# S5 increments as quarter-array products without a zero-padded token copy

## The chip, the cores and the metric

The program runs on one core of a Trainium2 chip. The metric is the device time of one execution in microseconds (us). Five engines work side by side, each through its own queue in order: TensorE (PE, with its weight loads shown apart as PEld), VectorE (DVE), ScalarE (ACT), GpSimd (POOL) and SyncE (SP, which here only issues transfers). PE's array has 128 rows (the contraction) and 128 columns (the rows of the output). A matmul that uses 64 of either leaves the rest to others: in the rows below `128*64` is a matmul that holds a stationary block of 128 rows and 64 columns, and `64*128` one of 64 rows and 128 columns.

## What is computed

Two network blocks run over 256 tokens of width 2048: an attention block with two layers, then a block whose mixer is a linear recurrence (S5). The part that matters:

```python
def s5_scan(u, lam_bar, b_bar, s0, reverse):
    bu = jnp.einsum('btgh,gph->btgp', u, b_bar)
    first = -1 if reverse else 0
    bu = bu.at[:, first].add(lam_bar * s0)
    a = jnp.broadcast_to(lam_bar, bu.shape)
    _, states = lax.associative_scan(_lin_rec_combine, (a, bu), axis=1, reverse=reverse)
    return states

def s5_mixer(h_ctx, h_lat, ...):
    u_ctx, u_lat = to_groups(h_ctx), to_groups(h_lat)
    ...
    for direction in range(2):
        st_ctx = s5_scan(uc_ctx, lam_bar, b_bar, s0, reverse)
        s_ctx_final = st_ctx[:, 0] if reverse else st_ctx[:, -1]
        st_lat = s5_scan(uc_lat, lam_bar, b_bar, s_ctx_final, reverse)
        y_lat = y_lat + jnp.einsum('btgp,ghp->btgh', st_lat, c_mat).real
```

Each of the 128 groups has 16 input features and 64 complex states, in two directions. The kernel takes four tokens together as a chunk (64 chunks in 256 tokens). A chunk's contribution to the state, its **increment**, is a product of 64 inputs (four tokens of 16 features) with a table of the group: 64 rows, and 64 states for each direction and for the real and the imaginary part. The recurrence then runs over the 64 chunks.

## The kernel before

Weights stream through SBUF in tiles of 128 columns, split into two parts (ACT makes `wh`, line 130; DVE makes `wl`, line 131), and are multiplied in three products (lines 156 to 158). The framework's scheduler sets the order of the instructions on every engine from its own model of their times, so an edit in one place can move instructions elsewhere.

The increments are made twice, both times by `chunk_inputs` (line 654), which handles a half block of 8 groups (a block is 16 groups; two tiles, `s` = 0 and 1, of 8 groups each, lie in the rows 0 to 63 and 64 to 127).

- **The context** (`ctx_states`, line 1245): a side job, cut into pieces that run between the weight tiles of the second attention layer, at 1036 to 1361 us of the profile. Eight blocks; in each, ACT scales the context's tokens into `ub` (line 1281, 16 instructions of 64x64), two half blocks of increments are made (line 665, table `wc`), ACT takes them out of PSUM (line 1289), and DVE folds the 64 chunks together (lines 1303 to 1306).
- **The latent tokens** (`s5_mix`, line 1312): at 1384 to 1600 us. The eight blocks are grouped in segments `S0` (blocks 0 and 1), `S1` (2 and 3), `S2` (4 and 5), `S3` (6) and `S4` (7). For each block the layer norm's last step (lines 1078, 1079) and the modulation (lines 1351 to 1353) give `u`; `to_chunks` (line 635) turns it on PE (lines 642 and 648, with copies at line 644 between) into `o2`, copies `o2` from PSUM to SBUF in two halves (line 651) and sends each half on by a DMA of SP (line 652); `chunk_inputs` makes the increments (line 665, table `wl`), and they are copied into the segment's state `S` (line 1363).

Then the recurrence runs in place on `S`, three instructions per chunk (lines 1380 to 1382): segment `S1` on POOL, the others on DVE, from `S0` on. A segment whose recurrence has ended is copied by ACT into `sn` (lines 1433, 1434) and multiplied with the output table (line 1439), on top of the products inside a chunk (line 1408); gelu, and a transposition (line 1470) follow, and then the GLU's weight tiles. The vector-matrix products of the modulations (line 195 on PE, line 210 on DVE, tiles `graw`) fill gaps throughout.

Before the change the increments use all 128 rows of the array: the tokens lie in `ub[128, 8, 2, 64]`, where for the rows of one tile the columns of the other are zero, so that one product gives both tiles' groups side by side:

```python
u = Ub[:, 4 * q + i]
nc.tensor.matmul(inc[ri][r, i], w[:, i, ri, r], u[:, :, ::-1] if d else u, start=True, stop=True)
```

One such matmul moves 128 columns (2 tiles, 64 chunks), half of whose inputs are zero. There are 16 in a half block: 4 group pairs `i`, 2 parts `ri`, 2 directions `d`. The two directions use the two column halves of the array. The profile counts two records for each of these matmuls, so a half block is `x32`. `inc[ri]` is one PSUM bank per part.

Of the kernel before, what the change touches and what calls it, by code (L numbers as in the profile page):

```python
# [11 lines left out]
F32 = mybir.dt.float32  # L12
# [89 lines left out]
def bc(ap, n):  # L102
    """ap [p, m] seen as [p, m, n], each element repeated n times."""
    return bass.AP(tensor=ap.tensor, offset=ap.offset, ap=[list(d) for d in ap.ap] + [[0, n]])


class K:
# [41 lines left out]
    def mm_t(self, a, order=range(KT)):  # L149
        """[128 columns, 256 tokens] of the next column tile; a[kt] = both parts of [128, 256]."""  # L150
# [10 lines left out]
    def mm_n(self, a, half):  # L161
        """[128 tokens, 2, 256 columns]: half 0 opens the sum with the first 8 kt, half 1 closes it."""
# [17 lines left out]
    def gemv(self, w, width, seg, c, outs, biases):  # L180
        """Generator: outs[i][128, 16] = c[i] @ w[:, 2048 seg:] + biases[i]; each step loads a chunk of 1 MB and
        yields the function that adds it, on the engine that send() names."""
# [63 lines left out]
    def step(self):  # L246
        """One step of the first side job."""
        while self.side and next(self.side[0], True):
            self.side.pop(0)
# [5 lines left out]
    def bg_add(self, *jobs):  # L255
        """Queue (name, generator): the first halves of all, then the second."""
        for _, gen in jobs:
            next(gen)
        self.bgq += [(name, gen, 8) for name, gen in jobs] * 2

    def policy(self, engines, split):
        """The engines that add the chunks, and which halves of the weights GpSimd splits."""
        self.pol = itertools.cycle(engines)
        self.spl = itertools.cycle(split)

    def bg(self, n=1, eng=None):
        """n steps of the vector products: each loads a chunk and adds the one before."""
# [25 lines left out]
    def rsqrt(self, v):  # L293
        """v[128, n] (positive) -> v ** -0.5: a guess from the exponent, a step of Newton's and one of Halley's."""
# [5 lines left out]
        # y = 3/8 of the better guess  # L300
# [9 lines left out]
    def spread(self, col, name="rb"):  # L310
        """col[128 tokens, n, 2] -> PSUM [128, n, 256], the value of each token in every partition."""
# [11 lines left out]
    def colsum(self, ps, src, first, last, cols=None):  # L323
        """ps[128 tokens, 2, n] += src[128, 256].T @ cols[128, n] (cols: ones)."""
# [6 lines left out]
    def bands(self, name):  # L331
        """PSUM [128, 256] of zeros for band()."""
# [7 lines left out]
    def band(self, g, q, cols, src):  # L340
        """Rows 32 q .. of g += cols[128, n].T @ src[128, 256]."""
# [3 lines left out]
    def band_sums(self, g, sel, name):  # L345
        """PSUM [128 tokens, 2, n]: the rows of g that sel[128, n] picks and adds."""
# [20 lines left out]
    def small_bg(self, out, a, b, c, d):  # L367
        """a * (1 + b) and c * (1 + b) + d (without c: d), by halves."""
# [16 lines left out]
    def affine_split(self, src, S, B, dst, js=range(KT)):  # L385
        """dst(kt) = both parts of src(kt) * S + B."""
# [13 lines left out]
    def s5_exp(self, x, t, em1=False):  # L400
        """x, t: lists of [128, 128] scratch; returns exp(x) (or exp(x) - 1) in t[0]."""
# [19 lines left out]
    def cmul(self, o, a, b, t):  # L421
        """complex pairs: o = a * b; t: four scratch tiles."""
# [12 lines left out]
    def s5_compact(self):  # L435
# [25 lines left out]
        # w = (lambda_bar - 1) / a  # L461
# [15 lines left out]
        # powers  # L477
# [5 lines left out]
        # factors of the tables by half blocks: [hb, table (W, V), ri, 8 groups, 4 tokens]  # L483
# [17 lines left out]
        # chunk decay and its squarings, per group ((re, im), (-im, re))  # L501
# [12 lines left out]
    def s5_prod(self, t, xr, xi, lr, li, part):  # L514
        """t = the two products of part 0 (real) or 1 (imaginary) of x * l, x [128, n, 16], l [128, n, 4]."""
# [9 lines left out]
    def s5_inputs_table(self, W):  # L525
        """Generator over half blocks (8 groups): the table W from a chunk's tokens to its state, in the
        workspace W[128, 4096]."""
# [39 lines left out]
    def s5_outputs_table(self, W):  # L567
        """Generator over half blocks: the tables V from a chunk's state to its outputs and M inside a
        chunk, in the workspace W[128, 4096]."""
# [4 lines left out]
        # C A^|lag| of 4 groups by lag -3 .. 3, zero where the lag is the other direction's  # L574
# [60 lines left out]
    def to_chunks(self, us, Ub, U, uc, dve=False):  # L635
        """us: two of [128 d, 256 tokens] -> U[128 (tile, tau, h), 8 groups, 64 chunks] (if any), and apart for
        the two tiles in Ub[128, 8 groups, 2, 64], whose other half is zero; uc(q): scratch [64, 4, 2, 64]."""
# [11 lines left out]
        for s in range(2):  # L649
            rows = slice(64 * s, 64 * s + 64)  # L650
            (v.tensor_copy if dve and s else nc.scalar.copy)(Ub[rows, :, s], o2[rows])
            nc.sync.dma_start(U[rows], Ub[rows, :, s])

    def chunk_inputs(self, w, Ub, q, evac):
        """w[128 (s, tau, h), 4, 2, 128 (dir, state)], Ub[128, 8, 2, 64], group pairs 4q .. 4q+3:
        evac(ri, psum[128, 8, 64]), the second direction's chunks backwards."""
# [3 lines left out]
        for i in range(4):  # L660
            for ri in range(2):
                for d in range(2):
                    r = slice(64 * d, 64 * d + 64)
                    u = Ub[:, 4 * q + i]
                    nc.tensor.matmul(inc[ri][r, i], w[:, i, ri, r], u[:, :, ::-1] if d else u, start=True, stop=True)  # L665
        for ri in range(2):
            evac(ri, inc[ri].rearrange("p i s c -> p (i s) c"))

# [77 lines left out]
    def consts(self):  # L746
# [17 lines left out]
        # the first of 32 columns  # L764
# [5 lines left out]
        self.ub = cp.tile([128, 8, 2, 64], F32, name="ub")  # L770
        nc.gpsimd.memset(self.ub, 0.0)
        # one-hot rows p % 16
        self.e16 = cp.tile([128, 16], F32, name="e16")
        nc.vector.tensor_reduce(self.e16, self.idn.rearrange("p (c h) -> p h c", h=16), axis=AX.X, op=ADD)
        # silu of the conditions
# [16 lines left out]
        # one-hot rows that pick the four bands of a vector product  # L792
# [10 lines left out]
        # lambda of the differential attention  # L803
# [10 lines left out]
        # distances s - t, with the future far away  # L814
# [161 lines left out]
    def ctx_rms(self):  # L976
        """1/rms of the context's tokens in the order of its chunks: rx[(tile, tau, h), chunk]."""
# [22 lines left out]
    def out_norm(self, o_, gate, ln, rms=False):  # L1000
        """x <- (z - mean) / std of z = alpha x + gate * (o @ w_out), summed about the mean of the first half
        of the features; with rms also PSUM [128, 256] of 1/rms of the layer norm's output."""
# [3 lines left out]
        if rms:  # L1006
            mw = self.vt.tile([128, KT, 3], F32, name="mw")           # 1, g^2, g b
            mq = self.vt.tile([128, 3, KT], F32, name="mq")           # g^2, g b, b^2
# [55 lines left out]
        if rms:  # L1064
            # sum of (g (w - m) r + b)^2
# [18 lines left out]
    def layer1(self):  # L1084
# [12 lines left out]
        def forget():  # L1097
            """Fs: both parts of the sums F of the log forget gates; nid: columns that pick -F of a head; FT: F's
            transpose."""
# [145 lines left out]
    def ctx_states(self, S, B):  # L1245
        """Generator: the context's last states, by blocks of 16 groups."""
# [7 lines left out]
        # scale and shift of the features in the order of the chunks' rows  # L1254
# [18 lines left out]
        for b in range(8):  # L1273
# [4 lines left out]
            for i in range(8):  # L1278
                for s in range(2):
                    r = slice(64 * s, 64 * s + 64)  # L1280
# [424 lines left out]
```

## Time and profile before

| | |
|---|---|
| time, median of 3 runs (lowest to highest) | 2597.3 us (2597.07 to 2597.63) |
| span of the profiled execution | 2600.7 us |
| PE busy | 2397.3 us (92%) |
| DVE busy | 1755.7 us (68%) |
| ACT busy | 1255.6 us (48%) |
| POOL busy | 209.7 us (8%) |

The span of the profiled execution lies 3.4 us (0.13%) above the median of the timed runs. Busy shares are means over stages that differ much: PE is nearly always busy while weight tiles are multiplied, and much less while the recurrence runs. What a change is worth is therefore read stage by stage, from a table of busy times in windows, and along the chain of work.

### The profile page before, as it was taken

What the parts mean: (1) busy time and instruction counts of PE and PEld (TensorE: products, weight loads), DVE (VectorE), ACT (ScalarE), POOL (GpSimd) and SP (SyncE); (2) the same over time, 40 slices, a digit from 0 to 9 for tenths busy, and PEclk for the clock granted to TensorE, in tenths of its full rate; (3) what the DMA queues carried; (4) which work ended last, traced back from release to release, by engine and by line L of the source; (5) the groups of instructions that cost most, each with busy time, mean ns of one, the idle gap of its engine ahead of it and who ended that gap; (6) DMA issues with size and microseconds to landing.
All of it is one profiled execution on the core that took longest, in us unless ns stands there. A gap on an engine that the chain in (4) does not pass through costs nothing.

```text
span 2600.7 us, 52283 instructions
## 1 busy us (share of the span) xinstructions
PE 2397.3 (92%) x20998; PEld 2172.4 (84%) x20998; DVE 1755.7 (68%) x3223; ACT 1255.6 (48%) x2178; POOL 209.7 (8%) x432
## 2 busy tenths in 40 slices
PE   5699999999899999999997445999899999999997
PEld 1299999999688888898886335998899999999996
DVE  3287878868766555788778998876754554555554
ACT  1455544444365565766555155544544443443442
POOL 0000000000011110000000853000000000000000
PEclk9699999999899999999998766999899999999998
DMA  9999999878779998788776543996355555555552
GB/s 330 343 337 318 333 329 329 317 253 326 252 248 339 333 328 289 264 279 283 258 232 204 182 165 120 331 318 238 119 184 183 184 184 182 186 180 186 182 179 94
DMA packets 203332, 644.92 MB, mean 248 GB/s; under 512 B 41009, under 2 KB 49457, under 8 KB 202705
## 3 DMA queue, kind: packets, MB, share of 16 engines
q1 hardware_dynamic: 195616, 620.47, 69.3%
q0 software_dynamic: 7472, 21.11, 2.1%
q8 instruction: 164, 2.69, 0.4%
q14 instruction: 80, 0.65, 0.1%
HBM read 613.71 MB, written 25.69 MB: 246 GB/s over the span
## 4 chain that ended last, share of the span: by engine, by line
PE 83%; DVE 10%; DMA 3%; ACT 3%; issue 1%; SPq 0%; DVEq 0%; POOL 0%; ACTq 0%
PE pj L156 22%; PE pj L157 21%; PE pj L158 21%; PE g L195 3%; DVE scan_t L1381 3%; PE pjv L173 3%; PE pjv L174 2%; DMA graw<-in_w_mod 2%; PE pjv L175 2%; DVE scan_t L1380 2%; DVE S L1382 2%; PE inc L665 1%; PE st L343 1%; PE kps L617 1%; PE ys L343 1%
## 5 line engine op out<-in xcount | busy, mean ns | idle before, releaser
L131 DVE TENSOR_TENSOR wl<-w,wh 128x1024 fp32r<-128x1024 f32 x638 | 777.6, 1224 | 533.7 <-ACT wh L130 526.0
L130 ACT CAST wh<-w 128x1024 fp32r<-128x1024 f32 x640 | 664.9, 1048 | 717.2 <-PE pj L157 414.0
L157 PE MATMUL pj<-h2L,wh 128*128 128x256 f32 x1024 | 291.1, 286 | 0.4 <-DVE h2L L393 0.3
L156 PE MATMUL pj<-h2H,wh 128*128 128x256 f32 x1024 | 286.8, 286 | 4.7 <-ACT h2H L392 3.6
L158 PE MATMUL pj<-h2H,wl 128*128 128x256 f32 x1024 | 290.7, 285 | 0.0
L156 PE MATMUL pj<-dH,wh 128*128 128x256 f32 x1024 | 290.1, 284 | 0.0
L157 PE MATMUL pj<-dL,wh 128*128 128x256 f32 x1024 | 289.9, 283 | 0.0
L158 PE MATMUL pj<-dH,wl 128*128 128x256 f32 x1024 | 289.9, 283 | 0.0
L210 DVE SCALAR_TENSOR_TENSOR gacc<-graw,csilu,gacc 128x1024 f32<-128x1024 f32 x207 | 264.7, 1279 | 26.0 <-DMA graw<-in_w_mod 16.5
L156 PE MATMUL pj<-hH,wh 128*128 128x256 f32 x768 | 221.5, 289 | 5.2 <-ACT hH L392 4.0
L158 PE MATMUL pj<-hH,wl 128*128 128x256 f32 x768 | 221.4, 289 | 0.5 <-DVE wl L131 0.5
L157 PE MATMUL pj<-hL,wh 128*128 128x256 f32 x768 | 221.1, 288 | 0.0
L195 PE MATMUL g<-graw,czc 128*32 128x256 f32 x1776 | 169.8, 466 | 51.3 <-DMA graw<-in_w_mod 49.9
L156 PEld LDWEIGHTS pj<-h2H,wh 128*128 128x128 f32 x1024 | 196.0, 194 | 5.7 <-ACT h2H L392 4.1
L157 PEld LDWEIGHTS pj<-h2L,wh 128*128 128x128 f32 x1024 | 198.6, 194 | 1.2 <-DVE h2L L393 1.2
L158 PEld LDWEIGHTS pj<-h2H,wl 128*128 128x128 f32 x1024 | 198.8, 194 | 0.1
L156 PEld LDWEIGHTS pj<-dH,wh 128*128 128x128 f32 x1024 | 196.8, 192 | 1.7 <-issue 1.7
L158 PEld LDWEIGHTS pj<-dH,wl 128*128 128x128 f32 x1024 | 196.8, 192 | 0.0
L157 PEld LDWEIGHTS pj<-dL,wh 128*128 128x128 f32 x1024 | 196.8, 192 | 0.0
L195 PEld LDWEIGHTS g<-graw,czc 128*32 128x32 f32 x1776 | 47.2, 120 | 130.5 <-DMA graw<-in_w_mod 105.5
L156 PEld LDWEIGHTS pj<-hH,wh 128*128 128x128 f32 x768 | 148.7, 194 | 8.8 <-ACT hH L392 4.1
L158 PEld LDWEIGHTS pj<-hH,wl 128*128 128x128 f32 x768 | 148.4, 193 | 4.5 <-issue 3.7
(476 smaller groups left out, 5907.6 us busy)
## 6 DMA issues: line engine op xcount, KB each, us to landing
graw<-in_w_mod SPq DMA_DIRECT2D x384, 512.0 KB, 5.7
w<-in_mlp_in SPq DMA_DIRECT2D x128, 512.0 KB, 3.5
w<-in_mlp_out SPq DMA_DIRECT2D x128, 512.0 KB, 3.6
w<-in_a_in SPq DMA_DIRECT2D x96, 512.0 KB, 5.9
graw<-in_w_kvmod SPq DMA_DIRECT2D x64, 512.0 KB, 6.0
w<-in_b_in SPq DMA_DIRECT2D x64, 512.0 KB, 5.8
w<-in_glu SPq DMA_DIRECT2D x64, 512.0 KB, 5.4
w<-in_a_v SPq DMA_DIRECT2D x32, 512.0 KB, 5.8
```

The source lines that it names most:

```text
L130: nc.scalar.copy(h, src)
L131: (eng or (nc.gpsimd if next(self.spl) else nc.vector)).tensor_sub(l, src, h)
L156: self.nc.tensor.matmul(ps, h, aH, start=kt == order[0], stop=False)
L157: self.nc.tensor.matmul(ps, h, aL, start=False, stop=False)
L158: self.nc.tensor.matmul(ps, l, aH, start=False, stop=kt == order[-1])
L173: self.nc.tensor.matmul(ps[:, i], aH[:, s], h, start=half == 0 and i == 0 and k == 0, stop=False)
L174: self.nc.tensor.matmul(ps[:, i], aH[:, s], l, start=False, stop=False)
L175: self.nc.tensor.matmul(ps[:, i], aL[:, s], h, start=False, stop=half == 1 and i == 1 and k == 7)
L195: nc.tensor.matmul(st["g"][32 * q:32 * q + 32], self.cz[c][:, ch * 2 + s], raw[s][:, q * 256:q * 256 + 256], start=st["n"] == 0, stop=ch = ...
L210: nc.vector.scalar_tensor_tensor(acc, raw[s], cc, acc, op0=MUL, op1=ADD)
L343: self.nc.tensor.matmul(g[32 * q:32 * q + n], cols, src, start=False, stop=False)
L1381: e.tensor_add(u, t[:, :, 0], s[:, :, :, c + 1])
```

## The change

`ub`, its clearing and its second buffer go. `to_chunks` copies `o2` once, as 128x512, straight to `U` (on DVE for segment `S0`, else on ACT). `ctx_states` scales the context's tokens in place in `u`, with 8 instructions of 128x64 a block in place of 16 of 64x64. `chunk_inputs` multiplies each tile's 64 rows apart: per half block 32 matmuls of 64 rows, 64 columns of weights and 64 moving columns, each in one quarter of the array (row half `s`, column half `d`), and `inc[s]` is one PSUM bank per row half. What leaves PSUM is the same amount, as every second group of `S` (or of the context's `inc`), both parts.

```diff
-        for s in range(2):
-            rows = slice(64 * s, 64 * s + 64)
-            (v.tensor_copy if dve and s else nc.scalar.copy)(Ub[rows, :, s], o2[rows])
-            nc.sync.dma_start(U[rows], Ub[rows, :, s])
+        (v.tensor_copy if dve else nc.scalar.copy)(U, o2)
...
         for i in range(4):
             for ri in range(2):
-                for d in range(2):
-                    r = slice(64 * d, 64 * d + 64)
-                    u = Ub[:, 4 * q + i]
-                    nc.tensor.matmul(inc[ri][r, i], w[:, i, ri, r], u[:, :, ::-1] if d else u, start=True, stop=True)
-        for ri in range(2):
-            evac(ri, inc[ri].rearrange("p i s c -> p (i s) c"))
+                for s in range(2):
+                    for d in range(2):
+                        g, r = slice(64 * s, 64 * s + 64), slice(64 * d, 64 * d + 64)
+                        u = U[g, 4 * q + i]
+                        nc.tensor.matmul(inc[s][r, i, ri], w[g, i, ri, r], u[:, ::-1] if d else u,
+                                         start=True, stop=True)
+        for s in range(2):
+            evac(s, inc[s])
...
-        self.ub = cp.tile([128, 8, 2, 64], F32, name="ub")
-        nc.gpsimd.memset(self.ub, 0.0)
...
             for i in range(8):
-                for s in range(2):
-                    r = slice(64 * s, 64 * s + 64)
-                    nc.scalar.activation(self.ub[r, i, s], u[r, i], AF.Identity, scale=sf[r, i, 0, b:b + 1],
-                                         bias=sf[r, i, 1, b:b + 1])
+                nc.scalar.activation(u[:, i], u[:, i], AF.Identity, scale=sf[:, i, 0, b:b + 1],
+                                     bias=sf[:, i, 1, b:b + 1])
...
-                def evac(ri, ps):
-                    nc.scalar.copy(inc[:, 8 * q:8 * q + 8, ri], ps)
-
-                self.chunk_inputs(w, self.ub, q, evac)
+                def evac(s, ps):
+                    nc.scalar.copy(inc[:, 8 * q + s:8 * q + 8:2], ps)
+
+                self.chunk_inputs(w, u, q, evac)
...
-        ub = [self.ub, self.ga.tile([128, 8, 2, 64], F32, name="ub2", tag="gacc")]
-        nc.gpsimd.memset(ub[1], 0.0)
...
-                self.to_chunks(us, ub[b % 2], U[:, b], uc, k < DVE_W)
+                self.to_chunks(us, U[:, b], uc, k < DVE_W)
...
-                    def evac(ri, ps):
-                        (v.tensor_copy if ri and k < DVE_W else nc.scalar.copy)(
-                            S[k][:, n0:n0 + 8, ri, 1:64], ps[:, :, 0:63])
-
-                    self.chunk_inputs(w, ub[b % 2], q, evac)
+                    def evac(s, ps):
+                        (v.tensor_copy if s and k < DVE_W else nc.scalar.copy)(
+                            S[k][:, n0 + s:n0 + 8:2, :, 1:64], ps[:, :, :, 0:63])
+
+                    self.chunk_inputs(w, U[:, b], q, evac)
```

The changed file is shorter by some comments, so its line numbers are a little lower: the increments are line 664, the copy to `U` line 649, the copies out of PSUM line 1357, the recurrence lines 1374 to 1376, the `sn` copies lines 1427 and 1428.

Since the scheduler decides the order, three places are shown. The first is PE's queue in the last context block (`pj` are the weight tiles' products, `st` and `g` sums of the layer norm and of a modulation; `inc<-ub,wc` becomes `inc<-uctx,wc`). Before:

```order
L343 MATMUL st<-xres,mw 3x256
L195 MATMUL g<-graw,czc_156 32x256 x8
L665 MATMUL inc<-ub,wc 64x128 x15
L343 MATMUL st<-zsq,mw 3x256
L343 MATMUL st<-xres,mw 3x256
L665 MATMUL inc<-ub,wc 64x128
L343 MATMUL st<-zsq,mw 3x256
```

After:

```order
L343 MATMUL st<-xres,mw 3x256
L195 MATMUL g<-graw,czc_154 32x256 x8
L664 MATMUL inc<-uctx,wc 64x64 x17
L343 MATMUL st<-zsq,mw 3x256
L343 MATMUL st<-xres,mw 3x256
L664 MATMUL inc<-uctx,wc 64x64 x2
L343 MATMUL st<-zsq,mw 3x256
L664 MATMUL inc<-uctx,wc 64x64 x13
```

The half block stands in the same place, as 32 narrow matmuls in three pieces instead of 16 wide ones in two.

The second is PE's queue in the first two blocks of the latent tokens (`o` are the transpositions; a half-clock stretch of the profile). Before:

```order
L665 MATMUL inc<-ub,wl 64x128 x32
L642 MATMUL o_16176<-idn,u_16163 64x8x16 x4
L648 MATMUL o_16183<-idn,uc 128x64 x4
L642 MATMUL o_16255<-idn,u_16243 64x8x16 x4
L648 MATMUL o_16183<-idn,uc 128x64 x4
L642 MATMUL o_16262<-idn,u_16249 64x8x16 x4
L648 MATMUL o_16269<-idn,uc 128x64 x4
L665 MATMUL inc<-ub_16068,wl 64x128 x32
L648 MATMUL o_16269<-idn,uc 128x64 x4
```

After:

```order
L664 MATMUL inc<-U,wl 64x64 x64
L642 MATMUL o_16393<-idn,u_16380 64x8x16 x4
L648 MATMUL o_16400<-idn,uc 128x64 x4
L642 MATMUL o_16501<-idn,u_16489 64x8x16 x4
L648 MATMUL o_16400<-idn,uc 128x64 x4
L642 MATMUL o_16508<-idn,u_16495 64x8x16 x4
L664 MATMUL inc<-U,wl 64x64 x64
L648 MATMUL o_16515<-idn,uc 128x64 x8
```

The increments of block 1 no longer stand behind half of the transpositions of block 2 (`o_16269`, now `o_16515`).

The third is ACT's queue at the end of the latent blocks (`S_16018` and `S_16019` are `S3` and `S4` before, `S_16208` and `S_16209` after; `S_16015` and `S_16205` are `S0`). Before:

```order
L1363 COPY S_16018<-inc 128x8x63 x4
L651 COPY ub_16068<-o_16697 64x8x64 x2
L1363 COPY S_16019<-inc 128x8x63 x4
L1433 COPY sn<-S_16015 64x1024
L1434 COPY sn<-S_16015 64x1024
```

After:

```order
L1427 COPY sn<-S_16205 64x1024
L1428 COPY sn<-S_16205 64x1024
L1357 COPY S_16208<-inc 128x4x2x63 x2
L1427 COPY sn<-S_16205 64x1024
L1428 COPY sn<-S_16205 64x1024
L649 COPY U<-o_17088 128x512
L1357 COPY S_16209<-inc 128x4x2x63 x4
```

The second half of `S3` now stands behind six of the eight `sn` copies of `S0` (four of them ahead of these rows), and the copy of block 7 and all of `S4` behind all eight. On DVE the recurrence of `S0` has 53 steps of its own at its start, where it had 25, before `S2` joins it; the number of DVE's recurrence instructions is the same.

## Rows read from the trace of the kernel before

**Rows 1.** The page: engines' busy time, and the chain of waits by engine.

```profile
PE 2397.3 (92%) x20998; PEld 2172.4 (84%) x20998; DVE 1755.7 (68%) x3223; ACT 1255.6 (48%) x2178; POOL 209.7 (8%) x432
...
PE 83%; DVE 10%; DMA 3%; ACT 3%; issue 1%; SPq 0%; DVEq 0%; POOL 0%; ACTq 0%
```

**Rows 2.** Windows: stretch, length; busy (instructions) of PE, PEld, DVE, ACT, POOL; clock; DMA; GB/s.

```profile
1044.50:1361.00 316.50, 313.76 (x2757) 276.47 (x2755) 252.82 (x455) 196.69 (x386) 6.97 (x16) 0.99 0.78 264
1361.00:1384.00 23.00, 19.09 (x155) 14.29 (x154) 19.14 (x57) 4.07 (x14) 0.47 (x1) 0.96 1.01 384
1384.00:1396.00 12.00, 7.06 (x36) 5.42 (x32) 11.66 (x37) 8.53 (x21) 1.31 (x3) 0.50 0.17 55
1396.00:1414.60 18.60, 15.38 (x161) 14.10 (x162) 11.16 (x29) 9.66 (x22) 0.00 (x0) 0.73 0.40 114
1414.60:1427.00 12.40, 11.31 (x166) 10.11 (x163) 11.10 (x40) 12.28 (x30) 0.59 (x2) 1.00 0.74 213
1427.00:1452.00 25.00, 22.93 (x370) 19.82 (x370) 23.66 (x66) 15.45 (x35) 21.11 (x52) 1.00 0.57 167
1452.00:1600.00 148.00, 62.40 (x878) 43.08 (x880) 146.66 (x619) 55.85 (x86) 91.75 (x172) 0.61 0.45 154
```

**Rows 3.** Windows of line 665 alone: stretch, length; busy of PE, PEld; clock; DMA; GB/s.

```profile
1044.50:1361.00 316.50, 36.64 (x512) 29.16 (x512) 0.99 0.78 264
1396.00:1452.00 56.00, 33.61 (x512) 31.68 (x512) 0.91 0.55 159
```

**Rows 4.** Timeline of PE, full clock: start, duration, line, out<-in, stationary, moving, records.

```profile
1357.95 1.97 PE L665 MATMUL inc<-ub,wc 128*64 128x128 f32 x32
...
1443.09 1.15 PE L1408 MATMUL y<-ml,U 128*64 128x64 f32 x32
...
1036.56 1.11 PE L1262 MATMUL sf<-ctx_ws,esel 128*64 128x16 f32 x32
...
911.05 0.59 PE L617 MATMUL kps<-gen_ws 128*32 128x112 f32 x16
```

**Rows 5.** Timeline of PE, one row half and both; window of the second.

```profile
1393.22 1.08 PE L648 MATMUL o<-idn,uc 64*128 64x64 f32 x8 [0.77 <-ACT u L1351]
...
1594.36 0.70 PE L1470 MATMUL zt<-idn,zb 64*128 64x64 f32 x8 [10.76 <-POOL zb L1459]
...
1594.00:1598.00 4.00, 3.64 (x56) 3.29 (x57) 3.76 (x8) 1.80 (x6) 2.98 (x4) 0.50 0.03 7
```

**Rows 6.** Waits at 1036 to 1350 us: who, for whom; us, times, longest.

```profile
ACT wh L130 <- PE pj L157: 69.6, 45, 5.0
...
DVE gacc L210 <- DMA graw<-in_w_mod: 10.5, 12, 2.7
```

**Rows 7.** The tile `ub`: instructions, shortest, median, longest ns, first to last start.

```profile
L1281 ACT ACTIVATE ub<-uctx,ctx_ws x128: 423/436/443, 1038.4 to 1318.4; 64x64 f32<-64x64 f32 x128
L652 SPq DMA_DIRECT2D U<-ub x16: 590/594/626, 1394.9 to 1444.9; - x16
L651 ACT COPY ub<-o x14: 564/581/602, 1394.3 to 1443.9; 64x512 f32<-64x512 f32 x14
```

**Rows 8.** Timeline of PE and DVE from block 0 to the first step of the recurrence.

```profile
1396.16 5.11 PE L665 MATMUL inc<-ub,wl 128*64 128x128 f32 x64 [0.86 <-DVE ub L651]
...
1406.35 0.69 DVE L651 COPY ub<-o 64x512 f32<-64x512 f32 x1
...
1406.91 0.69 PE L648 MATMUL o<-idn,uc 64*128 64x64 f32 x4 [1.04 <-ACT uc L644]
1407.53 6.22 PE L665 MATMUL inc<-ub,wl 128*64 128x128 f32 x64
...
1413.80 0.68 DVE L1363 COPY S<-inc 128x504 f32<-128x504 f32 x1 [1.87 <-PE inc L665]
1414.59 0.27 DVE L1381 TENSOR_TENSOR scan_t<-scan_t,S 128x64 f32<-128x64 f32 x1
```

**Rows 9.** Timeline of ACT: the first `sn` copy.

```profile
1504.10 1.04 ACT L1433 COPY sn<-S 64x1024 f32<-64x1024 f32 x1 [53.47 <-DVE S L1382]
```

More of the change, by code (lines that the diff above doesn't have):

```diff
@@ L633, in s5_outputs_table, with to_chunks @@
             yield
-    def to_chunks(self, us, Ub, U, uc, dve=False):
+    def to_chunks(self, us, U, uc, dve=False):
         nc, v = self.nc, self.nc.vector
@@ L648, in to_chunks, with chunk_inputs @@
             nc.tensor.transpose(o2[:, g], uc[g // 4][:, g % 4].rearrange("p s x -> p (s x)"), self.idn[:64, :64])
-        for s in range(2):
-            rows = slice(64 * s, 64 * s + 64)
-            (v.tensor_copy if dve and s else nc.scalar.copy)(Ub[rows, :, s], o2[rows])
-            nc.sync.dma_start(U[rows], Ub[rows, :, s])
-    def chunk_inputs(self, w, Ub, q, evac):
+        (v.tensor_copy if dve else nc.scalar.copy)(U, o2)
+    def chunk_inputs(self, w, U, q, evac):
         nc = self.nc
```

## The prediction

> **What bounds the kernel now.** I read the page first. PE is busy for 92% of the span, and the chain of waits lies on it for 83% [rows 1]; only where the chain leaves PE (10% on DVE) can something else set the time. So the second view is the table of windows [rows 2], which gives each stage its own limit.
>
> The context's increments lie at 1044 to 1361 us. There PE is busy 313.8 of 316.5 us at a clock of 0.99, DVE 252.8, ACT 196.7, and the DMA share is 0.78: PE alone is the limit, with 2.7 us of idle time in all. The waits say the same from the other side: ACT's largest wait is 69.6 us for PE's products, while DVE waits 10.5 us for modulation weights [rows 6]. A microsecond of PE work that goes here is a microsecond of the program, until another engine comes within reach, and the next, DVE, is some 60 us away.
>
> The latent increments lie at 1396 to 1452 us, in three different stretches. Until 1414.6 no engine is full: DVE 11.2 of 18.6 us, PE 15.4 at a clock of 0.73; it is a chain from copy to product to copy, and the last rows of it are the copy into `S` at 1413.80 and DVE's first step of the recurrence at 1414.59 [rows 8]. At 1414.6 to 1427 ACT is busy 12.28 of 12.40 us. From 1427 to 1600 DVE is the limit (23.7 of 25, then 146.7 of 148), and PE sits idle for more than half of the last stretch [rows 2]. So PE time saved after 1414.6 buys nothing by itself; what counts is when DVE's recurrence starts and how densely it runs.
>
> **Part 1, the price of a half block.** Line 665 costs PE 36.6 us in the context and 33.6 us on the latent side, 16 half blocks each (512 records at 32 a half block) [rows 3]. A half block in one piece takes 1.97 us: 32 records, which two column halves run side by side, so 16 steps. Line 1408 is the same shape with 64 moving columns in place of 128: also 16 steps, 1.15 us [rows 4]. The difference, 0.82 us over 16 steps, is 51 ns a step; a step is about 110 ns with 128 columns and 58 with 64, and some 0.21 us is the end of the last one.
>
> After the change a half block has 64 records with 64 moving columns. If all four quarters run side by side, that is again 16 steps, of 58 ns: 1.15 us. Nothing in this profile shows four quarters together, so I bound the step. Four column groups do run together: line 617 puts 16 records of 112 columns into 0.59 us, hence 4 steps of (0.59 - 0.21) / 4 = 95 ns [rows 4]. Two row halves run together as well: at the half clock, eight matmuls of one row half take 1.08 us (line 648), eight that are divided between both halves take 0.70 us (line 1470), both at a clock of 0.50 [rows 2, 5]. Column halves overlap, row halves overlap, and four groups overlap; I take the product of these, 58 ns. The lower bound for the step is this too: line 1262 moves only 16 columns, and its 16 steps take 1.11 us, as long as with 64 [rows 4], so something other than the moving columns already holds 58 ns. The upper bound is four one after another, 232 ns.
>
> In the context that is 16 x 0.82 = **13.1 us**, on the path. The pieces remain few and stand where they stood (three in place of two in the last block).
>
> **Part 2, what else changes in the context.** ACT's 128 scalings of 64x64 at 436 ns, 55.8 us in all [rows 7], become 64 of 128x64. If one takes as long as before, ACT is relieved of some 28 us; it was waiting for PE, so I cost this at nothing, and at most it recovers part of PE's 2.7 us idle. The in-place scaling means that the next product waits for all 128 rows of a group, which it did before too. The clearings on POOL, an engine that is 8% busy, are worth nothing.
>
> **Part 3, the start of the latent side.** The increments of block 1 begin at 1407.53, after a second copy on DVE (0.69 us from 1406.35) and after four transpositions of block 2 (0.69 us from 1406.91), and last 6.22 us at the half clock [rows 8]. After the change there is one copy of 128 rows, which I price at the 0.68 us of the 128x504 copy at 1413.80, and the transpositions stand behind. The products can start about 1.4 us earlier. At the half clock a step took (6.22 - 0.3) / 32 = 185 ns; a step of half the columns is at most the 107 ns by which line 648 steps at that clock (0.75 us over seven steps, the last one's 0.33 us left out) [rows 5], so 32 steps last 3.7 us, 2.5 less. The recurrence then starts 1.4 + 2.5, about **4 us** earlier. The ends: nothing, if DVE's own work ahead (the layer norm's last steps) is the later input; 6 us, if the clock is full by then.
>
> Against it stands the order. DVE now takes 53 steps of `S0` alone before `S2` joins, where it took 25. Alone, a step leaves DVE waiting for itself: 1.30 us idle in 12.4, then 1.34 in 25, against 1.34 in 148 once two segments interleave [rows 2]. With steps of 0.9 to 1.4 us that is some 0.09 us a step, and 28 more steps cost **2.5 us**. The latent side nets 1.5 us.
>
> **Part 4, what costs nothing, and its cover.** The other seven blocks' products save PE another 12 us at 1414 to 1452, where ACT and then DVE are full. The 16 DMAs from `ub` to `U` [rows 7] leave SP's queue; the loads of `wl` behind them are issued a little earlier, at a DMA share of 0.57 to 0.74, so without effect. ACT takes one copy a block in place of two of 0.58 us [rows 7], which loosens the stretch that ACT limits; `S1` comes to POOL sooner by 2 or 3 us, and POOL's recurrence ends well inside DVE's.
>
> **The sum.** 13.1 + 1.5 = 14.6 us. The profiled execution's 2600.7 us would become 2586.1; its span stands 3.4 us above the median of the runs, 2597.3, so the time is 2597.3 - 14.6 = **2582.7 us**. The range of this case alone: 1.5 us less in the context (pieces whose ends overlap less) and -5 to +6 on the latent side, some 2576 to 2590.
>
> **The rivals.** *The moved waits.* On ACT the second half of `S3` now stands behind six `sn` copies, which wait for the end of `S0`. The first such copy today starts at 1504.10 and takes 1.04 us, after ACT had idled 53 us for DVE [rows 9]. Six are 6.3 us, two copies into `S` more make 7.4, and DVE has about seven steps of `S2` (7 to 10 us) to do before it adds the first increment of `S3`. If `S2` runs faster than that, DVE stands still. PE, too, waits in its queue for block 7's copy, with modulation products behind it and their loads behind these. Up to 7.4 us of DVE's limit would go, and the 13 us of the context remain: 2582.7 + 6, about **2589**. For it: the margin is thin. Against: in DVE's queue the first addition of `S3` stands 24 instructions behind the last of `S0`, so most of the wait has work in front of it. Chance 0.12.
>
> *A floor per instruction.* No row shows more than one record in 24 ns (line 617: 95 ns for four; line 1408: 58 for two) [rows 4], and the quarters would need one in 14.5. If 24 is a floor, a half block takes 64 x 0.024 + 0.21 = 1.75 us, the context gains 16 x 0.22 = 3.5 us, and with 1.5 on the latent side the time is **2592**. Against it: line 617's 95 ns are fully explained by its 112 columns, since 64 columns take 51. Chance 0.08. The Trainium skill, in "TensorE: Matmul & The Clock Gate", section "Wait — 56ns, not 53.3ns?", states such a floor: start to start of matmuls never under about 25 ns, however small they are. By it the half block would take 1.8 us and the gain of the context would be under 3 us; the trace comes to 24 ns and neither confirms nor breaks it.
>
> *Row halves of one column half load one after another.* Then a step of four takes two of 58 ns, a half block 2.07 us, the context loses 1.6 us and the latent side about keeps its 1.5: **2597**, no change. Line 1470 speaks against it [rows 5], though it shows a transposition and at the half clock. Chance 0.05.
>
> *Slower.* The new shape is not overlapped at all: 64 records of 58 ns, 3.9 us a half block. The context gains 16 x 1.93 = 31 us, and block 1's products double at the half clock, another 7: about **2635**. It decides against the change from a step of 110 ns on. All three overlaps in rows 4 and 5 speak against it. Chance 0.05.
>
> **How the numbers follow.** The forecast has 0.70. A difference of 0.2%, 5.2 us, is about what a measurement of this kernel tells from none, so faster is below 2592.1. Faster: 0.70, 0.10 of the moved waits, 0.04 of the floor, 0.84. Same: 0.02 and 0.04 of these, 0.05 of the row halves, 0.11. Slower: 0.05. The range runs from 2574 (every end of the latent side in favour, and ACT's relief returning PE's 2.7 us) to 2592.5, which takes in the moved waits and half of the floor, and leaves out the cases of no change and of slower and small tails.
>
> **What would show it.** Right: a whole half block of `inc` in the context lasts 1.1 to 1.2 us, PE's busy time at line 664 in the context falls from 36.6 to about 23, and the second attention layer ends about 13 us earlier; the recurrence's first step follows block 0's first product by some 14 us instead of 18; DVE is still full to the end of the recurrence. A half block of 1.7 to 1.8 us means the floor, 2.0 the row halves, near 4 no overlap. DVE idle before the first step of `S3`, with ACT copying `sn`, means the moved waits. What would make me wrong without any of these is a DMA limit I don't see: the stretch at 1361 to 1384 runs at a share of 1.01 [rows 2], and if its loads can't start earlier by as much as PE does, it keeps part of the 13 us.

## The result

The changed kernel takes 2615.8 us (median of 4 runs, 2614.9 to 2618.4) where the kernel before takes 2597.5; the ratio is 1.0069, with a 95% interval of 1.0055 to 1.0084. It is 18 us **slower**, where 14.6 us faster was forecast. The profiled executions differ by less, 2613.1 against 2600.7 us, because the profile of before lies 3 us above its median and the one of after 3 us below; what follows works with differences between stretches, and with the timed runs for the sums.

The page and the windows of the changed kernel, to be held against [rows 1, 2]; the windows are cut at the recurrence's start and end and at a gap in PE's work (columns as in rows 2):

```profile
PE 2367.1 (91%) x22022; PEld 2147.9 (82%) x22022; DVE 1769.6 (68%) x3223; ACT 1215.9 (47%) x2106; POOL 203.0 (8%) x430
```

```profile
1402.60:1440.00 37.40, 24.50 (x806) 21.25 (x804) 34.17 (x102) 20.81 (x51) 15.58 (x40) 0.86 0.36 112
1440.00:1484.00 44.00, 0.00 (x0) 0.00 (x0) 41.91 (x122) 0.16 (x1) 36.58 (x89) 0.53 0.11 45
1484.00:1616.00 132.00, 58.65 (x1046) 41.98 (x1046) 125.85 (x537) 59.37 (x93) 57.67 (x96) 0.67 0.51 174
```

PE works 30 us less than before and the program is longer. Line 664 alone, in the context's stretch (length; busy of PE, PEld; clock; DMA; GB/s), and two of its pieces in PE's timeline:

```profile
1030.00:1353.00 323.00, 24.21 (x1024) 19.81 (x1024) 0.99 0.80 271
```

```profile
1340.93 0.79 PE L664 MATMUL inc<-uctx,wc 64*64 64x64 f32 x34
...
1350.04 0.81 PE L664 MATMUL inc<-uctx,wc 64*64 64x64 f32 x38
```

So the new shape does what it was priced at. PE's cost in the context falls from 36.64 us [rows 3] to 24.21, by 12.4 us (13.1 forecast). In the second piece 38 records begin within 0.81 us less the last one's 0.22: one in 16 ns. The four quarters run together.

The recurrence's first store is at 1403.0 us, 11.9 earlier than the same store before, and its last ends at 1616.0, 7.2 later. It takes 213 us where it took 194. That is the loss, and the waits on ACT and PE show what stands beside it. From the timelines of ACT and PE (the bracket is the idle time before, and who ended it):

```profile
1432.05 1.06 ACT L1357 COPY S<-inc 128x504 f32<-128x504 f32 x2 [0.20 <-PE inc L664]
1483.84 1.04 ACT L1427 COPY sn<-S 64x1024 f32<-64x1024 f32 x1 [50.73 <-DVE S L1376]
...
1493.39 0.58 ACT L649 COPY U<-o 128x512 f32<-128x512 f32 x1
```

```profile
1494.03 3.43 PE L664 MATMUL inc<-U,wl 64*64 64x64 f32 x128 [55.93 <-ACT U L649]
```

ACT waits 50.7 us for the end of `S0`, with block 7's copy behind it, and PE waits 55.9 us for that copy. Two causes offer themselves for the longer recurrence: **P**, the order on DVE, where `S0` now runs alone for 53 steps and only 72 steps hold two segments (100 before); and **W**, the waits that moved on ACT and PE. A third question is the context: PE saved 12.4 us there, and the layer norm behind it (`rb<-idn,ry`) comes only 9.4 us earlier, at 1378.5 instead of 1387.9.

### The profile page after: what moved, and what is told of

It is laid out like the page before. It is cut to its first block, busy times and chain, and to the rows that moved or that the text cites. A ratio compares the mean times of both kernels' runs of the same rounds, so it can differ in the third digit from the quotient of the medians.

```text
span 2613.1 us, 54223 instructions
## 1 busy us (share of the span) xinstructions
PE 2367.1 (91%) x22022; PEld 2147.9 (82%) x22022; DVE 1769.6 (68%) x3223; ACT 1215.9 (47%) x2106; POOL 203.0 (8%) x430
## 5 line engine op out<-in xcount | busy, mean ns | idle before, releaser
L157 PEld LDWEIGHTS pj<-hL,wh 128*128 128x128 f32 x768 | 149.1, 194 | 3.8 <-issue 3.7
```

Source lines behind the costliest of these rows:

```text
L157: self.nc.tensor.matmul(ps, h, aL, start=False, stop=False)
```

## Experiments

### Each half of the change alone

The context's half: `ctx_states` as changed, the latent side as before.

```diff
+    def chunk_inputs2(self, w, U, q, evac):
...
-                self.chunk_inputs(w, self.ub, q, evac)
+                self.chunk_inputs2(w, u, q, evac)
```

> Only the context's half of the change: its products in quarters and its scalings in place; the latent side as before, in the order of before on DVE and ACT. Theory P (the recurrence's order costs the time; a step of one segment alone takes nearly as long as a step of two): the context saves what it saved in the changed kernel, 10 to 12 us, and nothing is lost behind it, so about 2586 us. Theory D (the context's gain is itself eaten, by DMA or by DVE behind it): 2594 to 2598 us.

Measured: 2596.1 us against 2599.1, ratio 0.9985 (0.9976 to 0.9995), 3 to 4 us faster, in D's range: most of what PE saved does not arrive. The order on the latent side is that of before (25 steps of `S0` alone).

The latent half: the old wide products in the context, the changed `s5_mix`.

> Only the latent half of the change; the context as before. DVE and ACT then have the order of the changed kernel on the latent side (53 steps of S0 alone, the sn copies ahead of half of S3). Both theories that put the loss behind the start of the recurrence expect the whole loss without the context's gain: 2597 + 18 + 10, about 2626 us. If the loss came from the two halves together, it would be under 2616 us.

Measured: 2621.1 us, ratio 1.0084 (1.0069 to 1.0099), 22 us slower. That is 5 us under the 2626 expected, which had counted on 10 us of gain in the context, where the run above shows 3 or 4. The whole loss is on the latent side, and the halves add up: 22 less 3 or 4 is the 18 of both. In this kernel the recurrence takes 212.8 us.

### The order of the recurrence, written out

The recurrence of all DVE segments is written as a list of steps, and each of its instructions is tied behind the one before on DVE. The kernel before, with the changed kernel's list:

```diff
+SEQ = [(0,)] * 53 + [(0, 2)] * 10 + [(2,)] * 7 + [(2, 3)] * 46 + [(3,)] + [(3, 4)] * 16 + [(4,)] * 47
...
-            for c in range(63):
-                for s, ab, G, t, u in a:
+            for step in SEQ:
+                for op in range(3):
+                    for k in step:
```

> The kernel before, with its recurrence on DVE written out in the changed kernel's order: S0 alone for 53 steps where it was 25, 72 steps of two segments where there were 100. Nothing moves on ACT: all copies into S stand ahead of the sn copies, as before. Theory P: 28 steps of two become 56 of one; at 1.25 to 1.53 us (POOL at work) or 0.93 to 1.15 us (POOL done) that is 28 x 0.7 to 1.0 = 20 to 27 us, so 2617 to 2624 us. Theory W (the waits that moved on ACT and PE cost the time): about 2597 to 2600 us.

Measured: 2625.0 us, ratio 1.0093 (1.0077 to 1.0109), 24 to 26 us slower, 1 us above the range of P. Nothing else moved: all copies into `S` stand ahead of the `sn` copies, and block 7's products do not wait for them. P holds and W falls. The recurrence takes 213.7 us here, as in the changed kernel, and the rest of the program behind it 997.7 us, against 991.9 before. With this order the rest takes 994.0 to 997.7 us in three profiles (the latent half, the changed kernel, this one), that is 2 to 6 us more than before. With the order of before five kernels of this document have 989.5 to 992.8 us and the last one below 995.2. So the order seems to cost a few us behind the recurrence too; that `S4` alone at the end is the reason isn't shown.

The control is the kernel before with its own list written out.

```diff
+SEQ = [(0,)] * 25 + [(0, 2)] * 38 + [(2,)] + [(2, 3)] * 24 + [(3,)] + [(3, 4)] * 38 + [(4,)] * 25
```

> A control: the kernel before with its own order of the recurrence written out step by step, as the other written-out orders are. If the writing out itself costs nothing: 2597 to 2601 us, as the kernel before. If it costs something, it is part of the 26 us that the changed kernel's order cost when it was written into the kernel before.

Measured: 2601.2 us against 2598.5, ratio 1.0006 (0.9995 to 1.0018). The writing out costs nothing that can be told from zero, and at most 5 us by the interval, against the 24 to 26 us above.

The changed kernel with this list of before:

> The changed kernel, with its recurrence on DVE written out in the order of before (25 steps alone, then 100 of two, 25 alone at the end); the copies into S then stand ahead of the sn copies again on ACT. Theory P: the recurrence takes its 194 us from a start 12 us earlier, so about 2585 us, 30 us under the changed kernel. If the loss is elsewhere (PE at half clock, loads of the modulation's weights later): 2605 to 2616 us.

Measured: 2593.7 us against 2599.1, ratio 0.9981 (0.9971 to 0.9990). That is 23 us under the changed kernel (by the ratios, 0.0088 of 2598) and 5 us under the kernel before. This undoes the order and, on ACT, the moved waits together; with the run before, in which the order alone cost as much, the order was the loss. But the 14 us of gain that was to appear without it did not, only a third of it: neither theory had 2593.7 us.

**Why a step alone is so dear** is in DVE's timeline. The changed kernel while POOL is at work, three instructions to a step of one segment; then the kernel before in the same state, six to a step of two (x2 is one of each segment):

```profile
1450.14 0.39 DVE L1374 TENSOR_TENSOR scan_t<-S,scan_t 128x128 f32<-128x128 f32 x1
1450.57 0.47 DVE L1375 TENSOR_TENSOR scan_t<-scan_t,S 128x64 f32<-128x64 f32 x1
1451.07 0.44 DVE L1376 TENSOR_TENSOR S<-scan_t 128x64 f32<-128x64 f32 x1
1451.55 0.39 DVE L1374 TENSOR_TENSOR scan_t<-S,scan_t 128x128 f32<-128x128 f32 x1
```

```profile
1470.10 0.61 DVE L1380 TENSOR_TENSOR scan_t<-S,scan_t 128x128 f32<-128x128 f32 x2
1470.64 0.71 DVE L1381 TENSOR_TENSOR scan_t<-scan_t,S 128x64 f32<-128x64 f32 x2
1471.27 0.59 DVE L1382 TENSOR_TENSOR S<-scan_t 128x64 f32<-128x64 f32 x2
1471.74 0.61 DVE L1380 TENSOR_TENSOR scan_t<-S,scan_t 128x128 f32<-128x128 f32 x2
```

Alone, a step takes 1.41 us here, each instruction 0.39 to 0.47; with two segments 1.64 us for twice the work. Over whole stretches, with POOL idle in parts of them, it is 1.24 us a step for `S0` alone in the changed kernel (53 steps in 65.6 us), 1.54 for `S0` with `S2` before (38 in 58.7), 1.16 for `S3` with `S4` before, and 1.10 for `S4` alone in the changed kernel (46 in 50.5). Each instruction alone needs the result of the one before it, and DVE counts as busy for nearly all of that time. Two windows with POOL at work, `S0` alone in the changed kernel, then `S0` with `S2` before (the third busy time is DVE's):

```profile
1440.00:1468.50 28.50, 0.00 (x0) 0.00 (x0) 26.41 (x63) 0.00 (x0) 23.83 (x62) 0.54 0.17 69
```

```profile
1452.00:1498.00 46.00, 12.07 (x118) 3.14 (x118) 46.00 (x173) 0.00 (x0) 39.44 (x86) 0.56 0.52 174
```

Alone, DVE is busy for 93% of the time and begins 2.2 instructions in a microsecond; with two segments it is busy throughout and begins 3.8. The busy share shows 7% of a loss of some 40%. That the wait for the result before makes the difference is the reading that fits the price of a step with one, two and (below) three segments; no run separates it from another cost of a single chain.

A list with three segments at once, each with scratch of its own, in the changed kernel:

```diff
+SEQ = [(0,)] * 25 + [(0, 2)] * 38 + [(2, 3, 4)] * 25 + [(3, 4)] * 38
```

> The changed kernel with the recurrence written out so that S4 joins S2 and S3 as soon as S0 has ended (25 steps of S0 alone, 38 of two, 25 of three, 38 of two), each segment with scratch of its own. Theory P (a step alone is bound by the latency of its three instructions, a further segment in it costs about the instructions' own rate): the recurrence takes about 181 us in place of 194, less what the outputs of S3 and S4 now cost at the end (they end together): 2583 to 2590 us. If a third segment costs as much as a step of its own: 2592 to 2596 us.

Measured: 2598.0 us against 2598.5, ratio 1.0000 (0.9990 to 1.0009): no gain, a miss, above the ranges of both theories. The price of a step was right: 25 steps of three took 50.0 us, 2.0 us each, and the recurrence 180.2 us against 194.9 with the list of before. In the profiles what was lost is behind it, 1011.7 us against 991.4. This profile is that of the slowest of the kernel's twelve runs, 5.5 us above their median, and its recurrence also starts 5.5 us later than in the other; by the medians this kernel is 4 us slower than the one with the list of before. The windows from the recurrence's end on, this kernel and the one with the list of before:

```profile
1590.00:1625.00 35.00, 23.19 (x324) 21.66 (x324) 14.22 (x15) 26.52 (x44) 11.76 (x11) 0.78 0.42 137
```

```profile
1599.10:1634.00 34.90, 33.69 (x315) 31.22 (x315) 27.35 (x30) 25.14 (x41) 6.97 (x6) 0.94 0.72 253
```

`S3` and `S4` end together, ACT then has two blocks' outputs to make one after the other, and PE is idle for 12 of the next 35 us where it was idle for one. PE also did 4.6 us less of its work within the shorter recurrence (79.9 us busy against 84.4), and that work comes behind it. Some 5 of the 20 us behind the recurrence remain unexplained.

### What moved the order

In the scheduler's order `S0` has 25 steps of its own in the kernel before and with the context's half alone, 53 with the latent half alone. To part the shape of the matmul from the rest, the latent side was made with as many matmuls (64 columns each) and the same copies out of PSUM by halves, but over all 128 rows of the zero-padded tokens; the context in quarters.

```diff
-                        g, r = slice(64 * s, 64 * s + 64), slice(64 * d, 64 * d + 64)
-                        u = U[g, 4 * q + i]
-                        nc.tensor.matmul(inc[s][r, i, ri], w[g, i, ri, r], u[:, ::-1] if d else u,
+                        r = slice(64 * d, 64 * d + 64)
+                        u = U[:, 4 * q + i, s]
+                        nc.tensor.matmul(inc[s][r, i, ri], w[:, i, ri, r], u[:, ::-1] if d else u,
```

> The context in quarters as in the changed kernel; on the latent side the same 64 matmuls of 64 columns for each pair of half blocks and the same copies out of PSUM by halves, but over all 128 rows of the zero-padded tokens. The scheduler then gives S0 29 steps of its own in place of 53 and leaves the sn copies behind all copies into S. Theory P (the order costs the time): near the context's half alone, 2594 to 2600 us. If the new form of the copies out of PSUM or the number of instructions were the cost: 2610 us or more.

Measured: 2596.8 us against 2598.5, ratio 0.9994 (0.9984 to 1.0004). `S0` has 29 steps of its own, and the recurrence takes 197.8 us. So neither the number of matmuls nor the copies by halves cost the time. One more order tells the rest, of a kernel that was not run: the kernel before, with its zero-padded copy, its DMAs and its two copies a block, and with nothing but the latent products in quarters, already has `S0` alone for 53 steps. The products over 64 rows move the order by themselves. That the scheduler's model prices them above what they take on the chip is the likely reading, but no run shows it; the model itself was not looked into.

### The context

The stretch from the first increment of the context to the last product of the layer (length; busy of PE, PEld, DVE, ACT, POOL; clock; DMA; GB/s), for the kernel before, the changed one, the context's half alone, and the kernel with a fifth buffer (below), in this order:

```profile
1044.80:1375.10 330.30, 327.56 (x2872) 288.48 (x2875) 263.42 (x470) 197.97 (x391) 6.97 (x16) 0.99 0.79 269
```

```profile
1045.00:1366.40 321.40, 315.68 (x3384) 280.08 (x3387) 262.71 (x473) 162.80 (x325) 7.84 (x16) 0.99 0.81 277
```

```profile
1045.20:1374.80 329.60, 319.92 (x3383) 282.87 (x3386) 262.70 (x473) 161.78 (x325) 8.37 (x16) 0.97 0.79 270
```

```profile
1042.70:1360.30 317.60, 311.45 (x3365) 278.75 (x3367) 261.27 (x470) 159.30 (x316) 7.02 (x16) 0.99 0.80 275
```

PE's idle time (the length less its busy time) is 2.7 us before, 5.7 in the changed kernel, 9.7 with the context alone; there the granted clock is lower too (0.97 of full speed on average against 0.99), and the same matmuls count some 4 us more busy time than in the changed kernel. Of 12.4 us saved, 8.9 were left in one profile and 0.7 in the other; in the other kernels with the context in quarters, but for the one with the fifth buffer, 4 to 7. Such differences between single profiles are sure to some 3 us only: the four profiles with the context of before differ by 2.6 us in this stretch among themselves. The largest single gap is at 1241 us in the changed kernel. The waits around it, at 1215 to 1250 us (who, for whom; us, times, longest):

```profile
ACT uctx L1277 <- DVE uctx L1275: 9.2, 1, 9.2
DVE gacc L210 <- DMA graw<-in_w_mod: 6.6, 3, 2.9
...
PE pj L156 <- ACT oH L1208: 4.3, 1, 4.3
```

DVE waits in its queue for modulation weights; the product of the context's tokens with 1/rms (line 1275) stands behind that; ACT's eight scalings (line 1277) wait for the product, and `oH`, which the weight tiles' products need, stands behind the scalings. Over 1036 to 1350 us DVE's waits for `graw` come to 26.2 us in the changed kernel, 28.1 with the list of before and 29.5 with the context alone, against 10.5 [rows 6].

The first try moved the product with 1/rms ahead in the code:

```diff
-            v.tensor_mul(u, u, view(self.rx, 0, [[0, 8], [1, 64]]))
...
             yield
+            if b < 7:
+                v.tensor_mul(un, un, view(self.rx, 0, [[0, 8], [1, 64]]))
```

> The changed kernel with the recurrence in the order of before, and in the context the product of the tokens with 1/rms moved ahead by about half a block on DVE, so that ACT's scalings no longer wait in ACT's queue for a product that stands behind DVE's waits for modulation weights. Theory Q (PE's new idle time in the context, 4 to 6 us at one place plus half a clock behind it, comes from that wait): 5 to 8 us under the kernel with the order alone, so 2586 to 2589 us. If the lost time has another cause (DMA): 2592 to 2595 us.

Measured: 2595.6 us against 2598.5, ratio 0.9987 (0.9978 to 0.9996). No gain over the order alone. It says nothing about Q, because the scheduler put the product where it had been, behind the same waits (4.1 us for `graw` right before it), and the gap of PE was 5.4 us.

The second try gives the loads of modulation weights a buffer more:

```diff
-            self.rg = pool("rg", 4)
+            self.rg = pool("rg", 5)
```

> The changed kernel with the recurrence in the order of before, and a fifth buffer for the tiles of modulation weights (graw), which the context's tables (wc) share; it is 4 KB a partition, the room that the dropped zero-padded copy gave back. Theory D (the context's saved PE time turns into DVE's waits for graw, 10.5 us before and 26 to 29 us with the context in quarters, and with the work behind these in DVE's queue into PE's waits): DVE's waits for graw fall to 10 to 15 us, PE's idle time in the context to about 3 us, and the time by 4 to 8 us, 2586 to 2590 us. If buffers are not what these loads wait for: 2592 to 2596 us, with the waits where they were.

Measured: 2589.9 us against 2598.4, ratio 0.9970 (0.9961 to 0.9980), 8 us under the kernel before and the lowest of all here. The forecast time of D came; its mechanism did not: DVE's waits for `graw` at 1036 to 1350 fell only to 23.6 us, not to 10 to 15, and PE's idle time to 6.2 us, not 3. The context's stretch is 317.6 us, 12.7 shorter than before, but not because the idle time went: PE has 16.1 us less to do in it, 12.4 of them the increments and the rest other work, such as 16 records of the modulations' products (`g<-graw,czc`) that now fall outside the stretch. Against the order alone the buffer gives 3 to 4 us, and the two intervals overlap (0.9961 to 0.9980 and 0.9971 to 0.9990). So a gain from the buffer is likely and not shown, and the way from DVE's waits to the lost time in the context stays open. The buffer moves orders elsewhere too: behind the recurrence the program takes 995.2 us, about 4 more than with the order alone.

## Why the prediction was wrong

**Part 1, the price of a half block: right.** A step of the four quarters was put at 58 ns; that gives a saving of 13.1 us, and 12.4 were measured (24.21 us in place of 36.64). The floor of 24 ns for a record, the loads one after another and the lack of overlap are all out: a record began every 16 ns, and in the piece at 1350.04 us the starts come in groups of four, one group in 58 ns. The Trainium skill states a least distance of about 25 ns between matmuls, in "TensorE: Matmul & The Clock Gate", section "Wait — 56ns, not 53.3ns?"; for matmuls in different quarters the trace shows less, and the measurement decides.

**Part 2, what else changes in the context: wrong.** I costed it at nothing because PE alone was full and "the next, DVE, is some 60 us away". Busy time was the wrong measure of distance. DVE and ACT were far from full, but their queues run in order, and a product behind a load that comes late held up ACT and then PE; the timelines show this chain at one place, and no run proves it to be the whole cause. Of the 13.1 us, 3 to 4 arrived with the context's half alone and 1 to 9 in single profiles of the stretch. I had named a limit by loads as what would make me wrong, but put it at 1361 to 1384 us, and gave it no chance of its own.

**Part 3, the start of the latent side: near in the sum, not in its terms.** The first step came 11.9 us earlier, 8.7 of them because the context ended earlier; the remaining 3.2 stand against the 4 forecast. (The two kernels that differ from the one before only in how the recurrence is written out have that step at 1411.5 and 1411.8 us, so some 3 of the 11.9 us lie within the spread of single profiles.) In the changed kernel:

```profile
1386.34 3.69 PE L664 MATMUL inc<-U,wl 64*64 64x64 f32 x128 [0.41 <-DVE U L649]
...
1397.45 3.26 PE L664 MATMUL inc<-U,wl 64*64 64x64 f32 x111
...
1401.21 0.60 PE L664 MATMUL inc<-U,wl 64*64 64x64 f32 x17 [0.50 <-issue]
...
1402.65 0.27 DVE L1375 TENSOR_TENSOR scan_t<-scan_t,S 128x64 f32<-128x64 f32 x1
```

From block 0's first product to the first step it takes 16.3 us, where 18.4 were taken before and some 14 were forecast. Block 1's products begin 11.1 us after block 0's (11.4 before [rows 8]), so 0.3 us earlier and not 1.4; four transpositions of block 2 (line 642) still stand right ahead of them. The products last 4.4 us in place of 6.2, so 1.9 less and not 2.5. Even that is not the shape alone: the wide products of block 1 took 3.71 us in the kernel with the context's half alone, at a higher granted clock (0.81 from block 0's first product to the first step, 0.74 before). The last 1.1 us lie ahead of block 0's products, where nothing was forecast.

**Part 3, the order: the step that failed.** I saw that `S0` would run 28 steps more alone, and priced a step alone by DVE's idle share, 0.09 us, 2.5 us in all. The right price was in the same trace: 25 steps of `S0` alone took 30.7 us, 38 of two segments 58.7. To split one step of two into two steps alone therefore costs 2 x 1.23 - 1.54 = 0.92 us, mostly with POOL at work, and 28 of them some 26 us; the runs gave 19 to 20 us in the recurrence and 2 to 6 behind it, 22 to 26 in the timed runs. The sign of the whole prediction hung on this term, which was about ten times too small.

**The moved waits** came as described and far longer (50.7 us on ACT, 55.9 on PE), and cost next to nothing: with none of them, the order alone lost as much (24 to 26 us against the 22 of the latent half). Their price in the prediction was the wait of DVE before `S3`, which the profile shows as 0.7 us.

**The rivals and the range.** Slower had one rival, the lack of overlap, and its chance of 0.05 was all the chance that slower had. The range, 2574 to 2592.5, lies wholly on the wrong side; the ends of its costs on the latent side came from busy shares.

## What to carry to other kernels

In a chain of instructions in which each needs the one before, an engine's busy share says nothing of its throughput: compare how long a step takes with one chain and with two, and count the steps of each kind in the new order. When a scheduler sets the order, an edit may move steps on an engine that it doesn't touch, so the order has to be read and priced for every engine that is the limit later, and can be written out by hand where it got worse. When the bound engine is relieved in a stretch of in-order queues, look for the loads and the small products that its peers wait for, and count only what arrives at the end of the stretch. One profile of a kernel is sure to a few us here, so a gain of 3 us needs timed runs.

## What was not expected of the hardware

Records of matmuls in four quarters of the array begin every 16 ns on average, loads of the stationary block included. An instruction of the recurrence on DVE takes 0.27 to 0.29 us with POOL idle and 0.39 to 0.47 with POOL at work when it stands alone. The pair is slower with POOL at work as well. With POOL idle, a step of `S0` with `S2` before and one of a single segment of that size in the changed kernel:

```profile
1501.84 0.49 DVE L1380 TENSOR_TENSOR scan_t<-S,scan_t 128x128 f32<-128x128 f32 x2
...
1502.91 0.49 DVE L1380 TENSOR_TENSOR scan_t<-S,scan_t 128x128 f32<-128x128 f32 x2
```

```profile
1484.65 0.29 DVE L1374 TENSOR_TENSOR scan_t<-S,scan_t 128x128 f32<-128x128 f32 x1
...
1485.59 0.29 DVE L1374 TENSOR_TENSOR scan_t<-S,scan_t 128x128 f32<-128x128 f32 x1
```

The pair takes 1.07 us a step and the single segment 0.94; with POOL at work they take 1.64 and 1.41. Both take about half as long again, and in both states the second segment costs only 0.1 to 0.2 us a step.
